# Eleven gated activations of a decoder layer turned by DMA transposes of 16-bit halves

## The chip, the cores and the metric

The kernel runs on one core of one Trainium2 chip. The metric is the device time of one execution in microseconds (us). Engines are named as the profile names them: PE is TensorE's matmuls and PEld its weight loads, DVE is VectorE, ACT is ScalarE, POOL is GpSimd, SP is SyncE. A name with a q behind it (ACTq) is an engine's instruction queue, where DMAs are issued from.

## The reference

One layer of a decoder trunk on 256 rows of 2048 float32 values: a norm, three attention branches fed by one projection, gates, an output projection with a residual, a second norm, and a gated feed-forward part with a residual. The last part is what the change touches:

```python
h2 = rmsnorm(x, g_ffn)
gu = h2 @ w_gu
x = x + (jax.nn.silu(gu[..., :D_FF]) * gu[..., D_FF:]) @ w_down
```

`D_FF` is 5632, so `w_gu` has 2048 x 11264 values and `w_down` 5632 x 2048. All is float32.

## The kernel before

Matmuls take 32-bit values of reduced precision, so each float32 operand is split into a high half (a cast by ACT, L106) and a low half (the rest, a subtraction by DVE, L107). A product of two operands is three matmuls of 128x512: high by high (L162), low weight by high activation (L163), high weight by low activation (L164). Weights are loaded by SP in tiles of 128x1024 (`w_raw`, `g_raw`) and split into `w_hi` and `w_lo`, of which five buffers each go round.

The gated projection works on *pairs* of 512 columns, one of the gate half and one of the up half of `w_gu`; there are 11 pairs (`project_pair`, L318). Of the contraction's four chunks of 512 rows, two are done with seven products in place of eight (a Strassen form, `form`, which needs sums of weight tiles such as `u`, made by DVE at L303 and L314), and two plainly (`rest`). Results are gathered in PSUM tiles `ps`, `qs`, `z` and `v`. The order within a pair is X1, Y2, Z5, one plain step, X6, two plain steps, X7, a plain step, Z3, and so on; Z5 and X6 take their weights from `u`, X7 from `g_raw` with another `g_raw` added. X, Y are `ps` or `qs` in turn, Z and V are `z` and `v`. Copies of PSUM results into SBUF are `snapshot` (ACT, L298).

After a pair, ACT applies the gate's Silu (L811) and DVE multiplies with the up half (L812), into two tiles `sg` of 128 rows by 512 columns. The down projection needs them with columns on partitions. `to_a` does that as a *stage*, a generator that moves on by a step now and then while the next pair runs: four PE transposes of 128x128 into a PSUM tile `tr` (`transpose4`, L184), a copy by ACT (L802), and a store by POOL's DMA queue to `a_mem` in device memory (L803). `take_a` (L820) reads a chunk of four columns' blocks back as `a_raw` and splits it.

There are two queues of stages: `stages` moves on by a step at every weight split, `slow_stages` at every second one (`parts`, L284). Tiles named `sc` come from one pool of 12 buffers of 2 KB a partition (`scratch`). A scheduler that models time puts the instructions of each engine in their final order; `tc.keep_in_program_order` pins an instruction. Each engine runs its instructions in order, and so does each engine's queue issue DMAs.

Of the kernel before, what the change touches and what calls it, by code (L numbers as in the profile page):

```python
# [9 lines left out]

F32 = mybir.dt.float32
F32R = mybir.dt.float32r
AF = mybir.ActivationFunctionType
ALU = mybir.AluOpType
AX = mybir.AxisListType
# [3 lines left out]
P = 128  # L19
D = 2048  # L20
S = 256
NT = S // P
# [7 lines left out]
NB = 512  # L30
# [25 lines left out]
def hybrid_block(ctx: ExitStack, tc: tile.TileContext, x, g_mix, w_in, q_gain, k_gain, w_branch, w_out,  # L56
                 g_ffn, w_gu, w_down, rel_bias, onehot, extra, out):
    nc = tc.nc
# [20 lines left out]
    def pool(stack, name, side, bufs=1):  # L79
        return stack.enter_context(tc.tile_pool(name=name, bufs=bufs, side=side, reuse_waits="tile"))  # L80
# [5 lines left out]
    scratch = pool(ctx, "scratch", "right", 12)  # L86
    gx = pool(pgx, "gx", "right", 2)

    def half_kb(dt=F32):

        return scratch.tile([P, NB], dt, name="sc")
# [10 lines left out]

        tc.keep_in_program_order(nc.sync.dma_start(dst, src))

    def split(hi, lo, src):
        nc.scalar.copy(hi, src)  # L106
        nc.vector.tensor_sub(lo, src, hi.bitcast(F32))  # L107

    def weights(w, row0, nk, col0, fine):

        for c in range(0, nk, 2):
            raw = wpool.tile([P, 2, NB], F32, name="w_raw", bufs=4)
            hi = wpool.tile([P, 2, NB], F32R, name="w_hi")
            lo = wpool.tile([P, 2, NB], F32R, name="w_lo")
            src = w[row0 + c * P: row0 + (c + 2) * P, col0: col0 + NB].rearrange("(k p) n -> p k n", p=P)
            if fine and c < 4:
                for k in range(2):
                    nc.scalar.dma_start(raw[:, k, :], src[:, k, :])
                    split(hi[:, k, :], lo[:, k, :], raw[:, k, :])
                    yield c + k, hi[:, k, :], lo[:, k, :]  # L120
                continue
            nc.sync.dma_start(raw, src)
            split(hi, lo, raw)
            for k in range(2):
                yield c + k, hi[:, k, :], lo[:, k, :]


    stages, slow_stages = [], []
# [37 lines left out]
    def rsqrt_mean(dst, ss, n, cols):  # L166
# [3 lines left out]
        y = small.tile([P, cols], F32, name=f"rs_y{cols}")  # L170
        nc.scalar.activation(y, v, AF.Ln)
        nc.scalar.activation(y, y, AF.Exp, scale=-0.5)
        t = small.tile([P, cols], F32, name=f"rs_t{cols}")
# [6 lines left out]
    def transpose4(src):  # L180

        pt = tr.tile([P, 4, P], F32, name="tr")
        for i in range(4):
            nc.tensor.transpose(pt[:, i, :], src[:, i * P:(i + 1) * P], ident)  # L184
        return pt


    class Columns:


        def __init__(self, pl, name, nk):
            self.hi, self.lo = (pl.tile([P, nk, S], F32R, name=f"{name}_{n}") for n in ("hi", "lo"))

        def put(self, c, t, src):
            k, q = slice(4 * c, 4 * c + 4), slice(t * P, (t + 1) * P)
            split(self.hi[:, k, q], self.lo[:, k, q], src)
# [15 lines left out]
    class Sums:  # L212
# [8 lines left out]
        def place(self, pl, c):  # L221
            self.s[c] = [pl.tile([P, 4, S], F32R, name=f"{self.name}_s{n}{c}") for n in ("hi", "lo")]

# [14 lines left out]
    class Chunks(Sums):  # L238


        def __init__(self, pl, name, n, wc, alloc=True):
            super().__init__(pl, name, wc, False)
            self.t = {}
            if alloc:
                for c in range(n):
                    self.place(pl, c)

        def place(self, pl, c):
            if c in self.wc:
                super().place(pl, c)  # L250
                self.t[c] = [[pl.tile(sh, F32R, name=f"{self.name}_{t}{n}{c}") for n in ("hi", "lo")]
                             for t, sh in enumerate(([P, 4, P], [P, 2, P]))]
            else:
                self.t[c] = [pl.tile([P, 4, S], F32R, name=f"{self.name}_{n}{c}") for n in ("hi", "lo")]

# [157 lines left out]
    def squares(xc, dst, c):  # L413
        for t in range(NT):
            nc.scalar.activation(half_kb(), xc[t], AF.Square, accum_out=dst[:, t, c:c + 1])

# [85 lines left out]
    def stick_breaking(hl, qT, kT, v):  # L502
# [7 lines left out]
        l = pa.tile([P, n], F32, name="p", bufs=1)  # L510
        nc.scalar.activation(l, z[:, :n], AF.Abs)
        nc.scalar.activation(l, l, AF.Exp, scale=-1.0)
        nc.scalar.activation(l, l, AF.Ln, bias=1.0)
        sp = pa.tile([P, n], F32, name="pT", bufs=1)
# [281 lines left out]
    a_mem = dram.tile([NF // 4, P, 4, S], F32, name="a_mem")  # L796

    def to_a(c, srcs):
        for t in range(NT):
            pt = transpose4(srcs[t])  # L800
            st = half_kb().rearrange("p (k q) -> p k q", k=4)
            nc.scalar.copy(st, pt)  # L802
            nc.gpsimd.dma_start(a_mem[c, :, :, t * P:(t + 1) * P], st)  # L803
            yield

    for c in range(D_FF // NB):
        nxt = (h2, w_gu, (c + 1) * NB, D_FF + (c + 1) * NB) if c + 1 < D_FF // NB else None
        (g0, g1_, u0, u1), ahead = project_pair(h2, w_gu, c * NB, D_FF + c * NB, ahead, nxt)
        sg = [half_kb() for _ in range(NT)]
        for t, (g, u) in enumerate(((g0, u0), (g1_, u1))):  # L810
            nc.scalar.activation(sg[t], g, AF.Silu, scale=rstd2[:, t:t + 1])  # L811
            nc.vector.scalar_tensor_tensor(sg[t], u, rstd2[:, t:t + 1], sg[t], op0=ALU.mult, op1=ALU.mult)  # L812
        stages.append(to_a(c, sg))

    WD = (4, 6, 8)
    ORDER = [0, 1, 2, 4, 3, 6, 5, 8, 7, 9, 10]
# [3 lines left out]
    def take_a(pl, c):  # L820
        a.place(pl, c)
        raw = pr.tile([P, 4, S], F32, name="a_raw", bufs=2)
        nc.gpsimd.dma_start(raw, a_mem[c])
        if c in WD:
            t0, t1 = (raw[:, :, t * P:(t + 1) * P] for t in range(NT))
            a.put(c, 0, t0)
            a.put(c, 1, t1)
            a.put_sums(c, t0, t1, raw)
        else:
            split(*a.t[c], raw)  # L830
# [4 lines left out]
    pd = pool(ctx, "pd", "left")  # L835

    def take_rest():
        for c in ORDER[EARLY:]:
            take_a(pd, c)
            yield  # L840
            yield

    stages.append(take_rest())

    def down_pair(c0, mine, spare, queues):
# [124 lines left out]
```

## Time and profile before

| | us |
|---|---|
| median of three runs | 1436.16 (1434.45 to 1436.39) |
| the profiled execution | 1434.04 |
| its span, first to last instruction | 1432.3 |
| ACT busy in the span | 879.4 (61%) |
| DVE busy in the span | 1196.2 (84%) |

The profile is one execution. A row of a timeline gives the start in us from the span's beginning, the length in us, the engine, the line of the kernel, the operation, the tile written and the tiles read, the shapes, and in square brackets how long the engine stood idle before and what ended that. Equal instructions that follow each other are merged ("x2"), and their length is then that of all. A row of groups gives the total busy time and the mean in ns. A row of DMA issues gives the KB of one and the median us from its issue to its landing. Matmul lengths overlap: a 128x512 matmul is listed with 0.39 us, and the next starts 0.23 us after it.

The 22 evictions of L802 lie between 786.5 and 1208.1 us of the span. That is the stretch in which the gated activations are turned: the second pair to the eleventh, and the start of the down projection.

### The profile page before, as it was taken

The page shows a single profiled execution, that of the slowest core. Times are in us where ns is not written, and L with a number is a line of the kernel's source. Part 1 is how long each engine was busy: PE and PEld are TensorE (multiplying, and loading weights), DVE is VectorE, ACT ScalarE, POOL GpSimd, SP SyncE. Part 2 cuts the span into 40 slices and gives each one's busy share as a digit, 9 for nine tenths or more (in the row PEclk, how much of TensorE's full clock was granted, in tenths as well). Part 3 has the DMA queues.
Part 4 walks back from the last instruction along what each step waited for, and adds up shares of the span by engine and source line. Part 5 has one row for each costly group of instructions (what it writes and reads, how often), then busy time and mean ns, then how long its engine had stood idle before and what let it go on. Part 6 is the DMA issues. An engine that isn't in the chain of part 4 may idle for free.

```text
span 1432.3 us, 17776 instructions
## 1 busy us (share of the span) xinstructions
PE 1421.7 (99%) x6407; PEld 1172.9 (82%) x6407; DVE 1196.2 (84%) x1263; ACT 879.4 (61%) x1131; POOL 72.6 (5%) x133
## 2 busy tenths in 40 slices
PE   8999999999999999999999999999999999999998
PEld 6888888888878888888888888888888888888887
DVE  7788797866998887776689999999999998986775
ACT  6567866766766665444556666666666666654453
POOL 1000000000000002100100000000000010100000
PEclk9999999999999999999999999999999999999999
DMA  8763637475657667866686667566665766877552
GB/s 265 253 223 114 236 114 254 113 222 180 219 191 251 240 208 274 288 222 211 218 301 227 215 212 264 200 227 231 223 205 198 244 203 220 267 231 240 188 171 97
DMA packets 154472, 310.09 MB, mean 216 GB/s; under 512 B 10672, under 2 KB 12288, under 8 KB 154384
## 3 DMA queue, kind: packets, MB, share of 16 engines
q1 hardware_dynamic: 142624, 274.24, 57.5%
q0 software_dynamic: 10000, 32.62, 6.5%
q10 hardware_dynamic: 1760, 2.11, 0.4%
q8 instruction: 50, 0.82, 0.2%
q14 instruction: 38, 0.31, 0.1%
HBM read 292.65 MB, written 16.27 MB: 216 GB/s over the span
## 4 chain that ended last, share of the span: by engine, by line
PE 76%; DVE 5%; issue 2%; ACT 2%; DMA 1%; SPq 0%; DVEq 0%; ACTq 0%
PE qs L163 9%; PE qs L164 9%; PE qs L162 9%; PE ps L162 9%; PE ps L163 9%; PE ps L164 9%; PE z L164 4%; PE z L162 4%; PE z L163 4%; DVE w_lo L107 3%; PE v L162 2%; PE v L163 2%; PE v L164 2%; DMA w_raw<-in_w_gu 1%; PE tr L164 1%
## 5 line engine op out<-in xcount | busy, mean ns | idle before, releaser
L107 DVE TENSOR_TENSOR w_lo<-w_raw,w_hi 128x1024 fp32r<-128x1024 f32 (+1 forms) x338 | 409.0, 1216 | 94.5 <-ACT w_hi L106 91.0
L106 ACT CAST w_hi<-w_raw 128x1024 fp32r<-128x1024 f32 (+1 forms) x338 | 351.6, 1047 | 173.7 <-PE qs L164 67.3
L106 ACT CAST w_hi<-g_raw 128x1024 fp32r<-128x1024 f32 x184 | 192.4, 1052 | 122.3 <-PE ps L164 41.3
L107 DVE TENSOR_TENSOR w_lo<-g_raw,w_hi 128x1024 fp32r<-128x1024 f32 x184 | 219.8, 1223 | 35.0 <-ACT w_hi L106 34.2
L106 ACT CAST w_hi<-u 128x1024 fp32r<-128x1024 f32 x138 | 145.0, 1053 | 134.3 <-DVE u L303 64.3
L107 DVE TENSOR_TENSOR w_lo<-u,w_hi 128x1024 fp32r<-128x1024 f32 x138 | 166.6, 1223 | 36.9 <-ACT w_hi L106 35.5
L163 PE MATMUL ps<-w_lo,h_hi 128*128 128x512 f32 x368 | 143.8, 391 | 0.0
L164 PE MATMUL ps<-w_hi,h_lo 128*128 128x512 f32 x368 | 142.9, 390 | 0.0
L162 PE MATMUL ps<-w_hi,h_hi 128*128 128x512 f32 x368 | 140.2, 392 | 0.4 <-ACT h_hi L106 0.4
L163 PE MATMUL qs<-w_lo,h_hi 128*128 128x512 f32 x332 | 129.9, 391 | 0.8 <-DVE w_lo L107 0.8
L164 PE MATMUL qs<-w_hi,h_lo 128*128 128x512 f32 x332 | 129.4, 390 | 0.0
L162 PE MATMUL qs<-w_hi,h_hi 128*128 128x512 f32 x332 | 126.2, 391 | 0.0
L303 DVE TENSOR_TENSOR u<-u,g_raw 128x1024 f32<-128x1024 f32 x80 | 94.4, 1220 | 0.0
L162 PEld LDWEIGHTS ps<-w_hi,h_hi 128*128 128x128 f32 x368 | 69.0, 188 | 15.4 <-ACT h_hi L106 0.8
L164 PEld LDWEIGHTS ps<-w_hi,h_lo 128*128 128x128 f32 x368 | 69.1, 188 | 14.3
L163 PEld LDWEIGHTS ps<-w_lo,h_hi 128*128 128x128 f32 x368 | 69.1, 188 | 14.0
L163 PEld LDWEIGHTS qs<-w_lo,h_hi 128*128 128x128 f32 x332 | 62.4, 188 | 13.9 <-DVE w_lo L107 1.2
L164 PEld LDWEIGHTS qs<-w_hi,h_lo 128*128 128x128 f32 x332 | 62.3, 188 | 12.9
L162 PEld LDWEIGHTS qs<-w_hi,h_hi 128*128 128x128 f32 x332 | 62.3, 188 | 12.7
L314 DVE TENSOR_TENSOR u<-g_raw 128x1024 f32<-128x1024 f32 x40 | 48.9, 1223 | 22.9 <-DMA g_raw<-in_w_in 18.3
L162 PE MATMUL v<-w_hi,h_hi 128*128 128x512 f32 x120 | 47.5, 396 | 0.1
L303 DVE TENSOR_TENSOR g_raw<-g_raw 128x1024 f32<-128x1024 f32 x40 | 47.1, 1220 | 0.0
(376 smaller groups left out, 2914.8 us busy)
## 6 DMA issues: line engine op xcount, KB each, us to landing
w_raw<-in_w_in SPq DMA_DIRECT2D x118, 512.0 KB, 4.7
g_raw<-in_w_gu SPq DMA_DIRECT2D x88, 512.0 KB, 5.1
w_raw<-in_w_gu SPq DMA_DIRECT2D x88, 512.0 KB, 6.2
g_raw<-in_w_in SPq DMA_DIRECT2D x72, 512.0 KB, 6.0
w_raw<-in_w_down SPq DMA_DIRECT2D x64, 512.0 KB, 4.7
w_raw<-in_w_branch SPq DMA_DIRECT2D x32, 512.0 KB, 5.2
w_raw<-in_w_out SPq DMA_DIRECT2D x32, 512.0 KB, 4.7
g_raw<-in_w_down SPq DMA_DIRECT2D x24, 512.0 KB, 5.1
```

The costliest lines, as they stand in the source:

```text
L106: nc.scalar.copy(hi, src)
L107: nc.vector.tensor_sub(lo, src, hi.bitcast(F32))
L162: nc.tensor.matmul(ps, ah, wh, start=start, stop=False, **how)
L163: nc.tensor.matmul(ps, ah, wl, start=False, stop=False, **how)
L164: nc.tensor.matmul(ps, al, wh, start=False, stop=stop, **how)
L303: tc.keep_in_program_order(nc.vector.tensor_add(d, d, a))
L314: nc.vector.tensor_add(d, a, b)
```

## The change

The two `sg` tiles of a pair are no longer turned by PE. `turn_out` views a tile of 128x512 float32 as 128x1024 values of 16 bits, and ACT copies them apart into two planes (all low halves, then all high halves). A DMA transpose, issued from ACT's queue, turns the eight 128x128 blocks of these planes. `turn_in` lets ACT put the two halves together again into the float32 tile that POOL stores as before. No value is changed by this.

`to_a` issues the outgoing parts of both tiles in its first two steps and does the incoming parts in the next two. It is moved from `stages` to `slow_stages`, so that a step comes with every second weight split. `take_rest` gets two empty steps at its start.

`split` gets an argument `pin`, and `Chunks` an attribute of that name; no call passes the argument, and nothing reads the attribute.

```diff
+U16 = mybir.dt.uint16
...
-    def split(hi, lo, src):
-        nc.scalar.copy(hi, src)
+    def split(hi, lo, src, pin=False):
+        first = nc.scalar.copy(hi, src)
+        if pin:
+            tc.keep_in_program_order(first)
         nc.vector.tensor_sub(lo, src, hi.bitcast(F32))
...
+    def turn_out(src):
+
+        halves = scratch.tile([P, 2, NB], U16, name="sc")
+        nc.scalar.copy(halves, src.bitcast(U16).rearrange("p (n b) -> p b n", b=2))
+        turned = scratch.tile([P, 8, P], U16, name="sc")
+        nc.scalar.dma_start_transpose(turned, halves.rearrange("p b n -> p (b n)"))
+        return turned
+
+    def turn_in(dst, turned):
+
+        nc.scalar.copy(dst.bitcast(U16).rearrange("p k (q b) -> p b k q", b=2), turned.rearrange("p (b k) q -> p b k q", b=2))
...
     def to_a(c, srcs):
+        turned = []
         for t in range(NT):
-            pt = transpose4(srcs[t])
+            turned.append(turn_out(srcs[t]))
+            yield
+        for t in range(NT):
             st = half_kb().rearrange("p (k q) -> p k q", k=4)
-            nc.scalar.copy(st, pt)
+            turn_in(st, turned[t])
             nc.gpsimd.dma_start(a_mem[c, :, :, t * P:(t + 1) * P], st)
             yield
...
-        stages.append(to_a(c, sg))
+        slow_stages.append(to_a(c, sg))
...
     def take_rest():
+        yield
+        yield
         for c in ORDER[EARLY:]:
```

In the changed kernel the copies of `turn_out` are L193, its DMA transposes L195, and the copies of `turn_in` L200.

More of the change, by code (lines that the diff above doesn't have):

```diff
@@ L242, in __init__ @@
             super().__init__(pl, name, wc, False)
-            self.t = {}
+            self.t, self.pin = {}, not alloc
             if alloc:
```

## The prediction

> **What bounds the kernel now.** I read the page's busy times first, then the chain of waits, then the stretches of the gated projection, and last its timeline instruction by instruction.
>
> ```profile
> PE 1421.7 (99%) x6407; PEld 1172.9 (82%) x6407; DVE 1196.2 (84%) x1263; ACT 879.4 (61%) x1131; POOL 72.6 (5%) x133
> PE 76%; DVE 5%; issue 2%; ACT 2%; DMA 1%; SPq 0%; DVEq 0%; ACTq 0%
> 997.00:1039.00 42.00, 42.00 (x191) 34.82 (x190) 39.04 (x37) 26.82 (x31) 1.71 (x3) 1.00 0.64 216
> ```
>
> TensorE (PE) is never idle, and the last chain runs through it. The third line is one pair of the gated projection (columns: window, its length, then busy us and instructions of PE, PEld, DVE, ACT, POOL; clock, DMA share, GB/s): PE 42.00 of 42, VectorE (DVE) 39.04, ScalarE (ACT) 26.82, the DMA engines 64% busy. So a PE slot taken out is time gained, as long as the halves `w_hi` (from ACT) and `w_lo` (from DVE) arrive in time. Whether they do is read at the start of a pair, where their lead over PE is smallest:
>
> ```profile
> 865.26 1.41 DVE L812 SCALAR_TENSOR_TENSOR sc<-sc,rstd 128x512 f32<-128x512 f32 x2
> 865.76 1.06 ACT L106 CAST w_hi<-w_raw 128x1024 fp32r<-128x1024 f32 x1
> 867.99 2.35 DVE L303 TENSOR_TENSOR u<-u,g_raw 128x1024 f32<-128x1024 f32 x2
> 869.17 0.39 PE L164 MATMUL z<-w_hi,h_slo 128*128 128x512 f32 x1
> 869.32 1.05 ACT L106 CAST w_hi<-u 128x1024 fp32r<-128x1024 f32 x1 [2.50 <-DVE u L303]
> 869.40 0.39 PE L162 MATMUL v<-w_hi,h_hi 128*128 128x512 f32 x1
> 869.63 1.03 PE L184 MATMUL tr<-ident,sc 128*128 128x128 f32 x8
> 870.28 1.06 ACT L802 COPY sc<-tr 128x512 f32<-128x512 f32 x2
> 870.40 1.23 DVE L107 TENSOR_TENSOR w_lo<-u,w_hi 128x1024 fp32r<-128x1024 f32 x1
> 870.42 0.48 PE L163 MATMUL v<-w_lo,h_hi 128*128 128x512 f32 x1
> 870.74 0.40 PE L164 MATMUL v<-w_hi,h_lo 128*128 128x512 f32 x1
> 871.23 0.60 ACT L298 COPY sc<-z 128x512 f32<-128x512 f32 x1
> 871.65 0.40 PE L162 MATMUL ps<-w_hi,h_shi 128*128 128x512 f32 x1
> 871.88 0.40 PE L163 MATMUL ps<-w_lo,h_shi 128*128 128x512 f32 x1
> 871.71 1.07 ACT L106 CAST w_hi<-u 128x1024 fp32r<-128x1024 f32 x1
> 872.65 2.02 ACT L106 CAST w_hi<-w_raw 128x1024 fp32r<-128x1024 f32 x2
> 876.22 2.35 DVE L303 TENSOR_TENSOR g_raw<-g_raw 128x1024 f32<-128x1024 f32 x2
> 876.45 0.59 ACT L298 COPY sc<-ps 128x512 f32<-128x512 f32 x1 [1.77 <-PE ps L164]
> 877.53 2.13 ACT L106 CAST w_hi<-g_raw 128x1024 fp32r<-128x1024 f32 x2 [0.49 <-DVE g_raw L303]
> 878.62 2.36 DVE L107 TENSOR_TENSOR w_lo<-g_raw,w_hi 128x1024 fp32r<-128x1024 f32 x2
> 881.46 1.04 ACT L106 CAST a_hi<-a_raw 128x1024 fp32r<-128x1024 f32 x1
> ```
>
> (Start, length, engine, line.) The low half of the new `u` is ready at 870.40 + 1.23 = 871.63 and read at 871.88: 0.25 us of lead. I call this place the dip. A later pair already waits there:
>
> ```profile
> 914.27 0.50 PE L163 MATMUL qs<-w_lo,h_shi 128*128 128x512 f32 x1 [0.47 <-DVE w_lo L107]
> ```
>
> **Removed.** Eight transposes a pair, 22 x 4 = 88 in the 11 pairs. In the timeline they take PE from 869.63 to 870.42, 0.79 us, and the matmul behind them keeps its place 0.32 us (870.42 to 870.74) instead of the usual 0.23 (869.40 to 869.63): 0.88 us a pair, 9.7 us in all. That is the most that the change can win. The two evictions of L802 (1.06 us of ACT a pair) go too.
>
> A page of the Trainium skill, "VectorE: DVE Perf Modes", section "The three transpose paths", gives a 128x128 transpose of 16-bit values 390 ns on TensorE; the trace's 32-bit ones follow each other 0.1 us apart, so by the page's number alone the pair would win 3 us and not 0.88. The timeline decides.
>
> **Added on ACT.** Per pair, two taking-apart copies C0, C1 (L193 of the changed kernel, 128x1024 halves), two DMA transposes T0, T1 issued from ACT (L195), two putting-together copies I0, I1 (L200), each waiting for its transpose. Nothing shows a strided 16-bit copy; the nearest rows have as many elements (casts, 1.05 us, 0.96 from start to start: 2.02 for two) or as many bytes (L298, 0.59). I take 1.05. ACT has room on the average: 26.82 + 4 x 0.96 - 1.06 + two issues, under 33 of 41 us. Only the place of the work matters.
>
> What a transpose holds ACT's queue for (call it I) is not in the trace either. Bounds:
>
> ```profile
> 1.29 1.37 ACTq L118 DMA_DIRECT2D w_raw<-in_w_in  x3
> L803 POOL DMA_DIRECT2D a_mem<-sc x22 | 15.8, 730 | 402.3 <-ACT sc L802 402.2
> ```
>
> A plain DMA from ACT takes 1.37 / 3 = 0.46 us. POOL takes 0.73 us for a store of 512 rows of 512 B; a transpose moves 128 x 8 = 1024 rows of 256 B, at the same price a row 1.46 us. I take 1.46, since a transpose is made of such pieces.
>
> The built programs give the new order on ACT. In six pairs it is: last cast of `w_raw`, C0, T0, `u`, L298, C1, `u`, `w_raw`, `w_raw`, T1, I0, L298, I1, `g_raw`, `g_raw`. In all pairs PE now does the six `z` matmuls of the same `w_raw` between reading `w_hi` and `w_lo` of the first `u`. With the rows above: C0 866.7 to 867.8; T0 867.9 to 869.4, in which ACT stands still; first `u` 869.4 to 870.45 (869.32 before, for it waits for DVE's L303 anyway), its low half 870.5 to 871.7. PE needs the high half after six matmuls, 869.40 + 6 x 0.227 = 870.76, and the low one after six more, 872.35: both in time. L298 870.4, C1 870.95 to 871.95, second `u` to 872.9, its low half to 874.2; PE wants that at 872.35 + 8 x 0.227 = 874.2. High half of the next `w_raw` 873.85, wanted at 873.7. Waits of about 0.25 us: 0.88 - 0.25 = 0.63 won a pair, 3.8 us in six.
>
> In four pairs, the first ones, L298 and C1 stand ahead of both `u`. L298 waits for Z's last matmul (869.17 + 0.39), so C1 ends at 871.15, the first `u` at 872.1, its low half at 873.4 against 872.35: PE waits 1.05 us, and 0.25 at the next `w_raw`. These pairs wait some 0.3 now (from 0.25 of lead to 0.47 of wait): -0.88 + 1.3 - 0.3 = +0.1 each, +0.4 in four. The eleventh pair's transposes fall into the down projection, where ACT has less to do: -0.88.
>
> **Queued behind the new waits.** Behind I0 and I1 stand the `g_raw` casts, and behind these DVE and PE. T0 has from 867.9 to 874.8 until I0. T1 may start when C1 has ended (872.0), while ACT still works at casts; I1 stands behind L298, which waits for PE's last X6 matmul, so I1 starts about 876.3: 4.3 us after T1's start. `g_raw` is then cast at 877.3, DVE's L303 is done at 878.8, the low half at 880.0, and PE wants it at 881.46 (where the next `ps` product stood) - 0.88 + 0.25 = 880.8. Another 0.8 us is spare: T1 costs nothing up to 5.1 us. Landings that the trace shows for 256 KB:
>
> ```profile
> a_mem<-sc POOLq DMA_DIRECT2D x22, 256.0 KB, 2.5
> x<-sc POOLq DMA_DIRECT2D x8, 256.0 KB, 6.7
> ```
>
> I take the first, as it leaves the same tiles in the same stretch; with 1.46 of issue it makes 4.0.
>
> POOL's stores start 5 us later (I0's end), and three early pairs read their chunk right back; the cast of `a_raw` now stands in front of the next `u` casts, where ACT has been idle for 3.5 us. That covers it; without that cover the `u` casts would start later by what the load is late:
>
> ```profile
> 889.64 2.19 ACT L106 CAST w_hi<-u 128x1024 fp32r<-128x1024 f32 x2 [3.49 <-DVE u L303]
> 882.56 18.78 SPq L103 DMA_DIRECT2D g_raw<-in_w_gu  x8
> ```
>
> SP's loads that take over a transpose's semaphore are the next pair's `g_raw`, from 882.56: ten us after T1's start, no wait. T1 itself waits for the load of `b22`, which the `u` before it has already used. DVE does the same work. The `pin` argument is passed by nobody, and the two empty steps of `take_rest` move loads by two casts: nothing.
>
> **Sum.** -3.8 + 0.4 - 0.9 = -4.3 us. The profiled execution took 1434.04 us (span 1432.3 and 1.7 around it), so it would take 1429.7; the median of the three runs, 1436.16, lies 2.1 above it, and the forecast goes by the median: 1431.9, rounded 1432. With I of 0.46 the six pairs gain 0.15 more each: 1431; with no wait at all in the dip it is 1436.16 - 9.7 = 1426.
>
> **Rivals.** (a) The sequencer holds ACT longer, and the dip gives the gain back. For each 0.1 us of I above 1.46 the first `u` and everything to the second come 0.1 later, and PE with them: at 2.0 the six pairs wait 0.8 instead of 0.25 and win 0.1, sum 6 x -0.1 + 0.4 - 0.9 = -1.1, 1435. For: ACT stands empty during T0. Against: plain issues take 0.46. The Trainium skill has this rule: "DMA: Bandwidth & Descriptors", section "Why a DMA increments its semaphore by 16 and not by 1", in its table of earlier generations against a later one, puts an SBUF-to-SBUF transpose at 32 sequencer cycles a tile. For 64 tiles of 16x128 an estimate is 2048 cycles, 1.7 us at the 1.2 GHz which the skill's "Trainium Architecture — The Big Picture", section "The five engines, in one table", states for ScalarE, and -2.8 us for the sum instead of -4.3. Its 512 cycles for a plain DMA, 0.43 us, agree with the trace's 0.46.
>
> (b) Slower: T1 lands late, I1 blocks ACT ahead of `g_raw`, and PE waits at the X7 product. Place: the seven pairs where T1 is followed by I0, L298, I1. It decides from 5.1 us after T1's start, and each us beyond costs one us in seven pairs. At the longest landing row, 6.7 us: 7 x 1.6 = +11.2, 1443; with the issue's 1.46 on top, 7 x 3.1 = +21.7, 1454. For: the DMA engines are 64% busy with weights in the same window. Against: the 2.5 us row. The skill's section on the three paths gives the DMA's transpose of a single 128x128 1309 ns; T1 is eight of them, an estimate of 10.5 us if they go one by one, which would be far worse still, and 1.3 us if side by side.
>
> (c) Slower: copies that step over every second half cost twice a cast. Then C0 and C1 push the second `u` 2.1 us back and PE waits some 2 us in each of ten pairs: +20 - 4.3, 1452. For: no such copy is in the trace. Against: casts between two types run at one price, 1.05 to 1.07.
>
> **How the numbers follow.** Forecast 0.39, (a) 0.18, (b) 0.31, (c) 0.12. I count a change of 0.2%, 2.9 us, as the least that can be told from none: the forecast is faster, (a) the same but for a little, (b) and (c) slower: 0.40, 0.17, 0.43. The forecast's own range is 1426 to 1433. As (b) and (c) hold much, the range reaches up to 1449, past (b) at its row's end.
>
> **What would show it.**
>
> ```profile
> 994.63 0.59 ACT L802 COPY sc<-tr 128x512 f32<-128x512 f32 x1 [2.40 <-PE tr L184]
> 1036.37 0.59 ACT L802 COPY sc<-tr 128x512 f32<-128x512 f32 x1 [2.40 <-PE tr L184]
> ```
>
> Right: 88 transposes gone from PE, and a later pair's period shorter by about 0.6 us than the 1036.37 - 994.63 = 41.74 that two pairs' first evictions show now; L193 and L200 at 1.05 us; a transpose's issue near 1.5 us on ACT's queue and landing in under 5.1; ACT's wait before I1 ended by L298's `ps`, not by the DMA. (a) shows as waits of the `ps`/`qs` products of `u` for `w_lo` in every pair, (b) as ACT idle before L200 ended by a DMA, with DVE idle before the `g_raw` halves, (c) as 2 us for one copy. The forecast is wrong if PE's idle time in the pairs exceeds 0.9 us each.

## The result, and the profile after

The changed kernel takes 1449.09 us (median of 6 runs, 1440.68 to 1451.24) against 1435.31 for the kernel before (6 runs, 1433.76 to 1437.85): ratio 1.009, 95% interval 1.0075 to 1.0105. The sign of the forecast was wrong. The profiled execution has a span of 1449.0 us, 16.7 more than before.

First the page of the changed kernel: its busy times and the head of its chain of waits.

```profile
PE 1424.1 (98%) x6319; PEld 1165.0 (80%) x6319; DVE 1193.6 (82%) x1263; ACT 914.4 (63%) x1153; POOL 72.5 (5%) x133
...
PE 14%; DMA 1%; DVE 0%; ACT 0%; issue 0%; DVEq 0%
```

PE executes 88 instructions less and yet is busy 2.4 us longer; it is a hint that something made its instructions slower. The chain is followed back over some 15% of the span only, and a DMA takes a part of it. Now the view by line, of L193 (taking apart), L195 (the transposing DMA) and L200 (putting together); lengths are min/median/max in ns.

```profile
L193 ACT COPY sc<-sc x22: 1037/1044/1051, 782.5 to 1214.4; 128x1024 uint16<-128x1024 uint16 x22
...
L195 ACTq DMA_TRANSPOSE sc<-sc x22: 1247/1248/1393, 783.6 to 1215.5; - x22
...
  ACT sc L200: 17.0, 8
...
DMA to landing us min/median/max: 2.7/5.3/11.6
...
L200 ACT COPY sc<-sc x22: 1333/1366/1380, 790.3 to 1227.1; 128x1024 uint16<-128x1024 uint16 x22
```

A copy that reads every second half costs what a cast does, one that writes every second half 0.3 us more. An issue holds ACT's queue 1.25 us. What matters stands in the two lines between: the landing takes 5.3 us in the median and up to 11.6, and ACT stood 17.0 us before L200, in 8 of 22 cases. By the trace's landing times it is the first DMA of a pair, T0, that is slow: 6.4 us in the median of the eleven T0, 4.1 in that of the eleven T1. In the first ten pairs ACT waits six times, each time with I0 for T0 and never with I1 for T1; the last two of the eight waits are in the eleventh.

Where in the span the time goes is read from one instruction that both kernels have in each pair, DVE's product of gate and up half (L812 before, L830 after). Before and after, the fifth of them:

```profile
948.12 1.41 DVE L812 SCALAR_TENSOR_TENSOR sc<-sc,rstd 128x512 f32<-128x512 f32 x2
```

```profile
957.46 1.41 DVE L830 SCALAR_TENSOR_TENSOR sc<-sc,rstd 128x512 f32<-128x512 f32 x2
```

The changed kernel is 9.34 us late here. It was 0.66 early at the first pair; it is 9.03 late at the eleventh, and 16.52 late at PE's last matmul. So the first four pairs' transpositions, which run during the pairs two to five, cost 10.0 us, the six after them win 0.3, and the eleventh, in the down projection, costs 7.5. The same three figures are given for every run below. By stretches it is (columns as in the prediction; the DMA share sums the packets' times over 16 engines, and where packets overlap it can pass 1):

```profile
781.00:948.00 167.00, 159.20 (x677) 126.79 (x676) 147.96 (x140) 115.89 (x124) 7.38 (x11) 0.99 0.70 225
948.00:1200.00 252.00, 249.53 (x1086) 202.69 (x1085) 231.02 (x217) 177.35 (x193) 11.84 (x18) 1.00 0.74 228
1200.00:1245.00 45.00, 39.52 (x160) 31.20 (x159) 33.49 (x43) 28.77 (x33) 4.17 (x7) 0.92 0.80 212
```

PE is idle 7.8, 2.5 and 5.5 us in the three, and in the last its clock is 0.92 on the average. The two bad places follow, in the timeline of the changed kernel. The third pair, ACT first and then PE:

```profile
870.63 1.25 ACTq L195 DMA_TRANSPOSE sc<-sc  x1
...
877.75 1.34 ACT L200 COPY sc<-sc 128x1024 uint16<-128x1024 uint16 x1 [2.40 <-DMA sc<-sc]
878.96 1.98 ACT L107 CAST w_hi<-w_raw 128x1024 fp32r<-128x1024 f32 x2
...
875.71 0.51 PE L166 MATMUL ps<-w_lo,h_shi 128*128 128x512 f32 x1 [0.76 <-DVE w_lo L110]
...
878.15 0.40 PE L167 MATMUL ps<-w_hi,h_slo 128*128 128x512 f32 x1
880.04 0.50 PE L165 MATMUL v<-w_hi,h_hi 128*128 128x512 f32 x1 [1.50 <-ACT w_hi L107]
...
883.18 0.63 PE L167 MATMUL v<-w_hi,h_lo 128*128 128x512 f32 x1
883.60 0.63 PE L166 MATMUL z<-w_lo,h_hi 128*128 128x512 f32 x1
```

I0 stands directly behind the casts of `u`, ahead of both casts of `w_raw`. T0 lands 7.1 us after its issue; ACT waits 2.40, and PE 1.50 for the `w_hi` behind it. In the last lines matmuls follow each other 0.42 us apart instead of 0.23. In the six later pairs the order is another, and I0 comes 6.8 us after T0's issue instead of 4.7. Even so three T0 are later than that; the latest:

```profile
1085.66 1.25 ACTq L195 DMA_TRANSPOSE sc<-sc  x1
...
1094.94 1.37 ACT L200 COPY sc<-sc 128x1024 uint16<-128x1024 uint16 x1 [2.46 <-DMA sc<-sc]
```

The eleventh pair:

```profile
1215.47 1.31 ACTq L195 DMA_TRANSPOSE sc<-sc  x1
...
1219.99 1.35 ACT L200 COPY sc<-sc 128x1024 uint16<-128x1024 uint16 x1 [2.77 <-DMA sc<-sc]
...
1227.13 1.33 ACT L200 COPY sc<-sc 128x1024 uint16<-128x1024 uint16 x1 [4.88 <-DMA sc<-sc]
1228.34 1.03 ACT L107 CAST a_hi<-a_raw 128x1024 fp32r<-128x1024 f32 x1
...
1229.40 1.23 DVE L110 TENSOR_TENSOR a_lo<-a_raw,a_hi 128x1024 fp32r<-128x1024 f32 x1 [5.56 <-ACT a_hi L107]
1230.54 1.22 DVE L900 TENSOR_TENSOR u<-g_raw 128x1024 f32<-128x1024 f32 x1
...
1231.85 1.04 ACT L107 CAST w_hi<-u 128x1024 fp32r<-128x1024 f32 x1 [1.53 <-DVE u L900]
...
1232.94 0.79 PE L165 MATMUL v<-w_hi,a_shi 128*128 128x512 f32 x1 [5.22 <-ACT w_hi L107]
```

This is the chain: T1 lands 11.6 us after its issue, I1 waits for it, the cast of `a_raw` behind I1, DVE's subtraction behind the cast, `u` behind that on DVE, the cast of `u`, and PE. One thing does not show in it: the load of `a_raw`, issued by POOL at 1216.05, itself landed at 1227.77 (by the trace), 0.66 us after T1, so that without any wait for T1 the cast could have come only some 0.6 us earlier. PE stands still 5.22 us and then runs at half its clock (the last but two of the columns), as the view by short stretches shows:

```profile
1215.00:1227.00 12.00, 12.00 (x55) 9.94 (x54) 5.66 (x9) 4.48 (x6) 1.26 (x2) 1.00 1.11 170
1227.00:1233.00 6.00, 0.78 (x5) 0.32 (x3) 3.60 (x4) 4.33 (x5) 1.28 (x2) 0.97 0.53 189
1233.00:1239.00 6.00, 5.74 (x12) 3.74 (x13) 6.00 (x8) 3.33 (x5) 0.56 (x1) 0.50 0.85 305
1239.00:1245.00 6.00, 6.00 (x27) 4.78 (x26) 6.00 (x8) 6.00 (x7) 0.53 (x1) 0.96 0.45 148
```

In the third row twelve matmuls in six us instead of the 27 of the fourth: this gap costs its own length and some 3 us more. It is a part of why PE's busy time grew although it had less to do: by the trace's record of the clock the half clock holds for 6.8 us here and for 3.4 in the third pair, which makes some 5 us of matmul time.

### The profile page after: what moved, and what is told of

It is laid out like the page before. It is cut to its first block, busy times and chain, and to the rows that moved or that the text cites. A ratio compares the mean times of both kernels' runs of the same rounds, so it can differ in the third digit from the quotient of the medians.

```text
span 1449.0 us, 17624 instructions
## 1 busy us (share of the span) xinstructions
PE 1424.1 (98%) x6319; PEld 1165.0 (80%) x6319; DVE 1193.6 (82%) x1263; ACT 914.4 (63%) x1153; POOL 72.5 (5%) x133
## 5 line engine op out<-in xcount | busy, mean ns | idle before, releaser
L110 DVE TENSOR_TENSOR w_lo<-w_raw,w_hi 128x1024 fp32r<-128x1024 f32 (+1 forms) x338 | 407.7, 1215 | 107.4 <-ACT w_hi L107 104.5
L166 PE MATMUL ps<-w_lo,h_hi 128*128 128x512 f32 x368 | 144.0, 392 | 0.0
L166 PE MATMUL qs<-w_lo,h_hi 128*128 128x512 f32 x332 | 130.0, 392 | 0.8 <-DVE w_lo L110 0.8
L166 PEld LDWEIGHTS ps<-w_lo,h_hi 128*128 128x128 f32 x368 | 69.2, 188 | 14.0
L166 PEld LDWEIGHTS qs<-w_lo,h_hi 128*128 128x128 f32 x332 | 62.4, 188 | 13.9 <-DVE w_lo L110 1.2
L166 PE MATMUL v<-w_lo,h_hi 128*128 128x512 f32 x120 | 47.7, 398 | 1.6 <-DVE w_lo L110 1.6
```

Source lines behind the costliest of these rows:

```text
L166: nc.tensor.matmul(ps, ah, wl, start=False, stop=False, **how)
```

## The experiments

The first theories. L: the loss sits in two places, the four early pairs and the eleventh, where the wait for a landing stands on ACT ahead of casts that PE needs soon; the six pairs between gain. Q: a transposing DMA costs by itself wherever it stands, by its hold on ACT's queue and by its packets among the weight loads. All runs are given in this table. Each ratio is against the kernel before in the same round of runs. The last three columns are read from the profiled executions at the product of gate and up half, as above, against the one profile of the kernel before (minus is a gain). For the change they add up to 17.2 us where the medians differ by 13.8, since its profiled execution was one of its slower ones (1450.67) and that of the kernel before a quicker one (1434.04).

| run | median us | ratio to before, 95% interval | four early pairs | six later | eleventh |
|---|---|---|---|---|---|
| the change | 1449.09 | 1.0090 (1.0075 to 1.0105) | +10.0 | -0.3 | +7.5 |
| e1_last_by_pe | 1444.01 | 1.0053 (1.0034 to 1.0071) | +13.8 | -4.7 | +0.7 |
| e2_first4_by_pe | 1438.62 | 1.0024 (1.0014 to 1.0034) | +1.5 | -3.3 | +5.3 |
| e3_both_by_pe | 1432.62 | 0.9986 (0.9976 to 0.9995) | +0.7 | -2.1 | +0.5 |
| e4_no_wait | 1439.67 | 1.0036 (1.0024 to 1.0048) | +6.3 | -5.1 | +5.1 |
| e5_no_turn | 1449.57 | 1.0097 (1.0082 to 1.0112) | +10.5 | +3.2 | +1.8 |
| e6_last_by_dma_only | 1441.33 | 1.0041 (1.0026 to 1.0056) | +0.3 | 0.0 | +6.7 |
| e7_pause4_by_pe_last | 1443.52 | 1.0056 (1.0037 to 1.0075) | +8.0 | -0.7 | +0.1 |
| e8_pause3_by_pe_last | 1429.36 | 0.9955 (0.9938 to 0.9971) | -1.1 | -4.2 | +0.6 |
| e9_plain_copy | 1434.84 | 0.9996 (0.9986 to 1.0005) | +3.7 | -4.8 | +1.6 |
| e10_put_together_by_gpsimd | 1457.94 | 1.0153 (1.0138 to 1.0168) | +7.8 | +12.4 | +4.3 |
| e11_pause3_gpsimd | 1448.65 | 1.0089 (1.0074 to 1.0105) | +5.5 | +9.1 | +0.4 |

**Back to PE in one place, in the other, in both.** The old `to_a` is kept beside the new one as `to_a_pe` and takes some of the pairs: `c == 10` in e1, `c < 4` in e2, both in e3.

```diff
-        slow_stages.append(to_a(c, sg))
+        if c == 10:
+            stages.append(to_a_pe(c, sg))
+        else:
+            slow_stages.append(to_a(c, sg))
```

> The eleventh pair alone is turned by PE again, as in the kernel before; the ten others by DMA transposes. Theory L (late landing in two places): the changed kernel loses 7.5 us between the eleventh pair's start (9.0 us behind the kernel before) and the end (16.5 behind), because a transpose that shares the DMA engines with the down projection's first weights lands 11 us after its issue and ACT stands in front of it. Then this kernel wins those 7.5 us back: about 1441. Rival Q (ACT's added work, wherever it stands, is what costs): one pair of eleven comes back, 1/11 of 14 us, about 1448.

> Pairs one to four by PE, the seven others by DMA transposes. Theory L: the changed kernel is 10 us behind by its fifth pair, all of it in the four pairs where L298 and C1 stand ahead of both u casts and I0 ahead of the w_raw casts; this kernel wins 10 us back, about 1439, and keeps the eleventh pair's 7.5 us. Rival Q: 4/11 of 14 us come back, about 1444.

> Only the six pairs in the later order (five to ten) are turned by DMA transposes, the rest by PE. Theory L: both losses go, and the six pairs are about even: 1434 to 1436, within 0.2% of the kernel before, not the 3.8 us faster that the prediction's step had for these pairs, as I1 and I0 take 1.37 us instead of 1.05 and two of the six wait for a landing. Rival Q: 6/11 of 14 us stay, about 1443.

With the eleventh pair back on PE its loss of 7.5 us shrinks to 0.7, with the four early ones back theirs of 10.0 to 1.5, and with both the change wins 2.1 us (1434.71 before in these runs). e1 took 3 us more than L said, since its early pairs lost 13.8 and not 10.0: what a wait costs there differs from one build to the next. In e3 the gain is a little more than L expected. Q falls as a cost in every pair: with the same DMAs at the same places the six later pairs gain 2 to 5 us. The two empty steps of `take_rest` are in all these runs; with the eleventh pair on PE it loses 0.7 us at most, so they are not what it costs.

**The same loss without the ten other pairs.** The reverse of e1: `c < 10` goes to PE.

> Only the eleventh pair is transposed by DMAs, the ten before it by TensorE. If the loss in the down part is its own (theory L: the pair's two transpositions land under the burst of the first down weights, ScalarE's queue waits 4.9 us for the second, and TensorE runs out of weights and then runs at half clock for some us), the landmarks stay at 0 up to the start of the down projection, and the time is 5 to 8 us over the kernel before: about 1440 to 1443. If that loss needed the ten pairs before it (ScalarE and the queues already behind when the down projection begins), the time is within 2 us of before.

1441.33, in the range of L. Up to the start of the down projection the kernel runs with the kernel before (0.2 to 0.8 us early all the way), and then loses 6.7 us. The loss in the down projection is its own.

**No wait for the landing.** The putting together reads the planes as they were taken apart, not what the DMA has turned (so the activations stay unturned):

```diff
-            turn_in(st, turned[t])
+            turn_in(st, planes[t])
```

> All copies and transposes are issued as in the changed kernel, but the putting-together copies read the planes before the transpose, so nothing waits for a landing (the gated activations are left unturned). Theory L splits: the waits for landings go (the down projection's 7.5 us and some 4 of the 10 us in the early pairs), the wait of about 1.05 us for the first u in four pairs stays: 1436 to 1438. Rival Q: landings matter little, since ACT's work and the issue hold stay: 1446 or more.

1439.67: between the two. Against the change 8.8 us are gone of its 13.8 (13.78 - 4.96 by the medians and those before in the same runs), so the larger part of the loss is ACT's wait for landings. (By the start times, the order on ACT is that of the change in the ten pairs; in the eleventh I0 and I1 stand together, where the change has a cast between them.) The six later pairs now gain 0.84 each on the mean, nearly what the eight transposes are worth. But 5.1 us are still lost in the down projection, where L expected nothing. The timeline of this run, ACT:

```profile
1217.46 1.05 ACT L107 CAST a_hi<-a_raw 128x1024 fp32r<-128x1024 f32 x1 [4.49 <-DMA a_raw<-a_mem]
1220.99 1.04 ACT L107 CAST w_hi<-u 128x1024 fp32r<-128x1024 f32 x1 [2.48 <-DVE u L900]
```

The wait has moved: now the load of `a_raw` is late by 4.49 us, and the same chain over DVE follows. It lands 10.2 us after its own issue (11.7 in the change), 0.5 us after T1. PE stands still for 3.2 us, and 6.8 us of half clock follow, which is 3.4 of the 5.1. Whether the transpositions made the load late was the next question.

**No transposition at all.** The DMA of L195 is left out as well; both copies stay.

> All 22 transposing DMAs are left out, and the putting together reads the planes as they were taken apart (the output is not the reference's: the activations stay unturned); both copies of each half stay. Three theories. Traffic (X): in the down projection's beginning the transpositions' 256-byte packets hold the DMA engines in the stretch in which the first down weights and the a_raw chunks must come, and this, not the wait for a landing, makes the 5 us that were still lost there when nothing waited for a landing; then without them the down part loses under 1 us, and the time is about 1427 to 1431 (ten pairs without 8 transposes each, 0.6 to 0.9 us each, early pairs included). Hold (H): ScalarE's queue is held 1.25 us at each issue and this is what the early pairs lost in that run (+5.4 by the fifth pair); it is gone here too, so the fifth pair stands at or below 0. Order (O): what costs in the early pairs and in the down part is the two copies' own 4.8 us on ScalarE ahead of casts that TensorE needs soon, and then the early pairs still lose 3 us or more and the time stays at 1436 to 1440.

No theory holds whole: 1449.57, as slow as the change itself. The down projection loses only 1.8 us now, for X, though not under 1, and the load of `a_raw` lands after 4.9 us; but the early pairs lose 10.5 with no DMA in them, which fits the cause that O names but not its time. The timeline of ACT in this run (L198 is the putting together, L311 the snapshot):

```profile
874.03 1.04 ACT L193 COPY sc<-sc 128x1024 uint16<-128x1024 uint16 x1
874.98 0.58 ACT L311 COPY sc<-z 128x512 f32<-128x512 f32 x1
875.46 1.05 ACT L193 COPY sc<-sc 128x1024 uint16<-128x1024 uint16 x1
876.41 1.36 ACT L198 COPY sc<-sc 128x1024 uint16<-128x1024 uint16 x1
877.64 1.98 ACT L107 CAST w_hi<-u 128x1024 fp32r<-128x1024 f32 x2
```

The planner drew I0 ahead of both casts of `u` (in e4, where I0 waits for no landing either, it did not; why is not shown): 3.6 us of ACT in front of what PE needs next. It was not the experiment that it was meant to be, as the order changed with it. It shows that the place alone can cost as much as the whole change.

**A plain DMA in the transposition's place.** To keep the order, the DMA stays and only stops turning:

```diff
-        nc.scalar.dma_start_transpose(turned, halves.rearrange("p b n -> p (b n)"))
+        nc.scalar.dma_start(turned.rearrange("p b n -> p (b n)"), halves.rearrange("p b n -> p (b n)"))
```

> The changed kernel with a plain DMA from tile to tile (2 KB from each partition, the same 256 KB) in the place of each transposing one, issued from the same queue at the same places (the output is not the reference's: the activations stay unturned). If it is the transposing DMA itself that costs (T: ScalarE's queue held 1.25 us for each, 1024 packets of 256 bytes among the weight loads), its issues hold the queue under 0.2 us, the wait for the landing falls by half, and the time drops from 1449 to 1438 or less. If it is the place of the copies and of the waits on ScalarE ahead of casts that TensorE needs soon (O), only about a microsecond for each early pair goes, and the time stays at 1443 or over.

1434.84, with 1435.65 before: T holds, but for the hold of the queue, which is 0.47 us and not under 0.2, and O falls. By the start times the order on ACT is that of the change in the ten pairs; in the eleventh C1 comes one cast of `a_raw` earlier. The view of L195 in this run:

```profile
L195 ACTq DMA_DIRECT2D sc<-sc x22: 472/472/522, 784.1 to 1203.5; - x22
...
  ACT sc L200: 1.4, 2
...
DMA to landing us min/median/max: 2.2/2.9/5.4
```

The issue is 0.78 us shorter, the landing, counted from the issue's start, 2.9 instead of 5.3 us, and ACT's wait before L200 1.4 instead of 17.0. With the same 256 KB, the same copies and nearly the same order the 14 us are gone. The table's last columns divide the loss by cause and place. From the change to e4, the wait for landings: 3.7 us in the early pairs, 4.7 in the six later, 2.4 in the eleventh. From e4 to e9, what the transposing DMA does beside that, by its hold of the queue and by its transfer: 2.6, nothing, 3.5. In the eleventh it is the transfer: the load of `a_raw` that is issued beside T1, from POOL's queue, lands 5.3 us after its issue here, as against 10.2 in e4 and 11.7 in the change (5.5 in the kernel before). PE's gap is then 1.5 us instead of 3.2, and no half clock follows. What e9 keeps, +3.7 and +1.6, goes with the place of the copies, the short waits that are left and the later stores. Each figure is from single profiled executions, and e1's early pairs show that they can be 4 us off.

**The same DMAs in the middle of a pair.** Empty steps in `to_a` (4 and 2 of them in e7, as here, 3 and 3 in e8), and the eleventh pair by PE as in e1:

```diff
+        for _ in range(4):
+            yield
         for t in range(NT):
             turned.append(turn_out(srcs[t]))
             yield
+        for _ in range(2):
+            yield
```

> In the ten first pairs the taking apart and the issues start four steps of the planner later and the putting together two steps later still, so that they fall in the middle of the next pair, where the casts stand 3 to 5 us ahead of TensorE; the eleventh pair is transposed by TensorE. If the cost is only where the copies stand in ScalarE's order (L), each of the ten pairs gains the 0.88 us of its eight transposes less little, and the time is 1427 to 1430, faster than the kernel before and than the version with only the six later pairs. If the transposing DMAs cost by themselves (their packets delay weight loads wherever they stand, Q), it is 1433 or over.

> As the run before, but with three empty steps ahead: the first half is taken apart among the casts of g, the second between two casts of w_raw, and both are put together one after the other ahead of the casts of u. By L the gain depends on the slack where the two puttings together stand, 2.7 us in a row: 1427 to 1432, not better than the run before; by Q 1433 or over.

One step of the planner apart, and 14 us: e8 takes 1429.36, as L said, faster than both kernels (5.6 us under the kernel before); e7 takes 1443.52, as Q said. Neither holds as it stood. First ACT in e7, where a single pair loses 7.5 us and the nine others are about even:

```profile
844.32 1.91 ACTq L195 DMA_TRANSPOSE sc<-sc  x1
...
856.39 1.35 ACT L200 COPY sc<-sc 128x1024 uint16<-128x1024 uint16 x1 [4.95 <-DMA sc<-sc]
857.61 3.87 ACT L107 CAST w_hi<-g_raw 128x1024 fp32r<-128x1024 f32 x4
868.84 1.05 ACT L107 CAST a_hi<-a_raw 128x1024 fp32r<-128x1024 f32 x1 [7.35 <-DMA a_raw<-a_mem]
```

T1's first packet starts 4.4 us after the issue and its last one 11.4, while other transfers keep the DMA engines 79% busy (from the trace's packets); in the other nine pairs of e7 T1 ended after 5.2 to 9.1 us. T0 has the same place in both runs; T1 comes 9.1 us after T0 in e7 and 3.4 in e8, where both issues stand among the casts of `g_raw`:

```profile
1000.16 1.25 ACTq L195 DMA_TRANSPOSE sc<-sc  x1
...
1003.59 1.25 ACTq L195 DMA_TRANSPOSE sc<-sc  x1
1004.30 2.00 ACT L107 CAST w_hi<-g_raw 128x1024 fp32r<-128x1024 f32 x2
...
1008.58 2.58 ACT L200 COPY sc<-sc 128x1024 uint16<-128x1024 uint16 x2
```

Nine of its ten T1 have their first packet 1.2 us after the issue and their last one at 2.25 to 2.33, with the DMA engines otherwise nearly idle (some 2% busy); all landings of the run take 2.7 to 4.9 us, and L200 never waits. So the transposition is not slow by itself. It is slow when it is issued behind or among a burst of weight loads, and where the burst stands differs by a few us within a pair.

In the ten pairs e8 wins 5.3 of the 8.8 us that eighty transposes are worth; PE still waits 2.3 us between 781 and 1245.

**The putting together on GpSimd.** To take the wait off ACT, `turn_in` uses `nc.gpsimd.tensor_copy`, in the change (e10) and in e8 (e11).

> The changed kernel with the putting together, and so the wait for the landing, on GpSimd instead of ScalarE; the taking apart and the issues stay. By the theory that ScalarE's wait and 1.37 us of copy ahead of casts are the loss (W), the early pairs lose under 3 us instead of 9.4, the later ones gain 0.5 to 0.9 each, and the down part still loses some 5 us to the loads that come late there: about 1436 to 1440. By the theory that the taking apart and the issue alone, ahead of the casts of u, already lose what was lost (A), the fifth pair stands at +6 or over, and the time at 1443 or over. GpSimd's copy is not in any trace so far; if it takes over 10 us or takes VectorE's port, VectorE's subtractions get longer than 1.22 us and the time goes over 1450.

> The version that beat both (three empty steps ahead, eleventh pair by TensorE) with the putting together on GpSimd. There the ten pairs gained 5.2 us of the 8.8 that eighty transposes were worth; if ScalarE's 2.6 us of putting together ahead of the casts of u is what keeps back the rest, the time is 1426 to 1428; if it is the transpositions' packets, it stays at 1429; if GpSimd's copy disturbs VectorE, it is over 1432.

Both are slower than what they were made from, by 9 and 19 us, and the last case of each expectation came true. Neither W nor A is decided by e10: A's two signs came true (the fifth pair at +7.0, the time over 1443), but DVE's loss, which follows, would bring them about as well. The timeline of e10, DVE and then POOL:

```profile
878.51 2.35 DVE L110 TENSOR_TENSOR w_lo<-w_raw,w_hi 128x1024 fp32r<-128x1024 f32 x2
880.78 4.70 DVE L318 TENSOR_TENSOR g_raw<-g_raw 128x1024 f32<-128x1024 f32 x2
885.41 1.21 DVE L110 TENSOR_TENSOR w_lo<-g_raw,w_hi 128x1024 fp32r<-128x1024 f32 x1
...
879.86 2.22 POOL L200 COPY sc<-sc 128x1024 uint16<-128x1024 uint16 x1 [38.09 <-DVE w_lo L110]
...
883.02 1.43 POOL L200 COPY sc<-sc 128x1024 uint16<-128x1024 uint16 x1
```

Two DVE operations of 1.22 us take 4.70 while POOL copies: each is 1.1 us longer, nearly the length of an undisturbed copy of POOL (1.36, the shortest of the run), and POOL's first copy is 0.9 longer in turn. On DVE, which after PE had the least room, this is 2.3 us a pair. The Trainium skill, "SBUF — State Buffer", section "SBUF: two separate sides", says that DVE with two SBUF inputs and GpSimd share a pair of ports which one of them holds for a whole instruction while the other is blocked. The rows agree.

## Why the prediction was wrong, point by point

**Removed: right.** Without waits for landings (e4) the later pairs gain 0.84 each, near the 0.88 of the transposes and more than the 0.63 that the prediction left after waits at the dip.

**Prices of what was added on ACT: nearly right.** C 1.04 for 1.05, the issue 1.25 for 1.46, I 1.37 for 1.05. The rule of the Trainium skill of 32 sequencer cycles a tile ("DMA: Bandwidth & Descriptors", section "Why a DMA increments its semaphore by 16 and not by 1"), by which the estimate was 1.7 us, is too dear here: the row says 1.25. Rivals (a) and (c) fall with these rows.

**The landing: the term that was mis-sized.** "I take the first, as it leaves the same tiles in the same stretch; with 1.46 of issue it makes 4.0." It is 5.3 in the median and 11.6 at the longest. For T1, to which the sentence was applied, 4.0 was about right (4.1 in the median). T0 was given 6.9 us of room, "T0 has from 867.9 to 874.8 until I0", and no landing of its own was set against it: it takes 6.4 in the median and 7.4, 8.5 and 9.3 in three of the six later pairs. The row of 2.5 us was that of POOL's stores, at another moment of the pair. The mistake was to take a median of a row for a price, where the landing depends on what the DMA engines have to do in the us around the issue. The row of 64% was quoted and used only as an argument for a rival.

**The early pairs, +0.4 forecast, +10.0 measured: the step that failed first.** The waits at the dip were found about as worked out (PE's step at L166 in the third pair is 1.26 us instead of 0.23, where 1.05 of wait was forecast). But the order of the six later pairs was taken for what follows: "T0 has from 867.9 to 874.8 until I0." In three of the four early pairs I0 stands ahead of the two casts of `w_raw`, and ACT comes to it 4.7 us after the issue. With a landing of 7.1 us the wait goes straight through to PE. Then half clock adds to it: from 881 to 885 the granted clock is 0.57. This and the mis-sized landing are 3.7 of the ten us by e4; 2.6 more are hold and transfer by e9, for which the sum had only the issue's place in ACT's order; the 3.7 left are mostly the copies ahead of the `u` casts, worked out at +0.1 a pair (1.3 less 0.3 less 0.88), and +0.9 in e9.

**The eleventh pair, -0.88 forecast, +7.5 measured: the step with no working of its own.** "The eleventh pair's transposes fall into the down projection, where ACT has less to do". The stretch was never opened. It is where the first weights of `w_down` and chunks of `a_raw` are loaded beside T0 and T1: the DMA share of the stretch from 1215 to 1227 is 1.11 in the row above, at only 170 GB/s. T0 and T1 land after 7.8 and 11.6 us there, and the load of `a_raw` beside them after 11.7; the sum had a price for neither. "The two empty steps of `take_rest` move loads by two casts: nothing" holds, by the runs with the eleventh pair on PE.

**The six later pairs, -3.8 forecast, -0.3 measured.** The reasoning about their order holds: with no wait for landings they gain 5.1, in e9 4.8, in e1 4.7. In the change itself three landings of T0 came too late, as the waits between 948 and 1200 us say (total us, times, longest):

```profile
ACT sc L200 <- DMA sc<-sc: 4.7, 3, 2.5
```

**Rival (b)** had the mechanism, a landing later than 5.1 us that blocks ACT, and a span of times, 1443 to 1454, which holds the result. Its place was wrong: it had I1 wait for T1 in the pairs whose T1 is followed by I0, the snapshot and I1. There the waits are I0's for T0 and took back 4.7 us; most of the loss was in the other pairs, and I1 waits in the eleventh alone. So it is in part luck that its span of times holds the result. It was the better forecast all the same, as 64% DMA share stood in its favour and nothing but one row against it. The Trainium skill's 1309 ns for one 128x128 block ("VectorE: DVE Perf Modes", section "The three transpose paths") gave 10.5 us one by one and 1.3 side by side; with idle DMA engines the packets of all eight pass in 1.06 us (2.25 - 1.19 in e8), so they do not go one by one at that price. A sentence of the Trainium skill in "Advanced Engine Details and Errata", section "X-Bar Transpose (TRN2)", says that on TRN2 transposing DMAs are as fast as regular ones. e9 does not agree with it for transfers under load: 5.3 us against 2.9, of which 0.8 is the longer issue. With idle DMA engines it is 2.7 against 2.2, which the issue alone explains.

What stays open: how the 2.6 us of the early pairs between e4 and e9 divide between the hold of the queue and the transfer, and whether the transposition's small packets are what makes it slow among loads. No run changed one of them alone.

## What to carry to other kernels

A DMA on the path of an in-order engine is priced by the DMA share in the few us around its issue and by what is ahead of it in its own queue, not by the median landing of another queue's transfers; the transposing one here, of 1024 packets of 256 bytes, landed after nearly twice the time of a plain one, and it delayed the loads beside it. Put its issue where the engines are empty and its consumer where the casts behind it have slack: the same DMAs were worth -5.3 us in one place of the pair and +7.3 (nearly all in one pair) in another, one step away. And open the window of each exception, the first, the last and the odd pair, before a sum multiplies the price of the regular one: here 17.5 us came from five pairs whose order or whose neighbours were not those of the pair that was worked out.

## What the runs showed of the hardware

A gap of PE can cost more than its length. After 5.22 us of idling the clock was 0.50 for six us; in the third pair it was 0.57 for four us after waits of 0.24, 0.76 and 1.50 us between 874 and 881 and at the end of one of 0.52. The Trainium skill ("TensorE: Matmul & The Clock Gate", Part 1) ties the half clock to an idle window of 3.4 us; the first case agrees, the second has no single wait of that length. Nor have single gaps of 2.6 us in e6 and 3.2 in e4, after which the clock was 0.50 for 6.8 us; while a gap of 1.5 us in e9, and ten of 0.7 to 1.2 in e5, were followed by no half clock. The length of one gap does not decide it in these runs.

The same transposing DMA landed in 2.7 us and in 11.6, its first packet 1.2 us after the issue or 4.9. Two things differ between these cases: the load of the DMA engines, and what is ahead in ACT's queue. In seven of the eleven pairs of the change T1's first packet starts within 0.15 us of the end of T0's last, and in the eleventh 1.3 us after it, so T1 also waits for T0. A plain DMA of the same bytes stayed between 2.2 and 5.4.

A 16-bit copy of 128x1024 on ACT with every second element in its output costs 1.37 us, with every second one in its input 1.04. And in e10 a copy on GpSimd nearly doubles DVE's two-input operations beside it, from 1.22 to 2.35 us.
